# One load instead of two at the end of a streamed mixture of softmaxes, and a store and a wait moved by one step

## The chip, the core and the metric

The kernel runs on one core of one Trainium2 chip. The metric is the device time of one execution in microseconds (us); less is better. Engines are named as in the profile: ACT (ScalarE) computes the exponentials, DVE (VectorE) the weighted sums, POOL (GpSimd) one small product for each group of heads, and SP (SyncE) issues most of the transfers. The transfers themselves run on 16 DMA engines that all queues share.

## The reference

The input `logits` has 32 x 128 rows of 4 heads by 4096 values in float32 (268.4 MB); `prior` has 4 values for each row. Each row's four softmaxes are mixed with weights that are themselves a softmax:

```python
prior_probs = np.exp(prior - prior.max(axis=-1, keepdims=True))
prior_probs = prior_probs / prior_probs.sum(axis=-1, keepdims=True)
softmax = np.exp(logits - logits.max(axis=-1, keepdims=True))
softmax = softmax / softmax.sum(axis=-1, keepdims=True)
mixture = np.sum(prior_probs[..., None] * softmax, axis=2)
```

The output has 4096 rows of 4096 float32 values (67.1 MB). The kernel takes the exponentials without the subtraction of the maximum.

## The kernel before

The 4096 rows are cut into U = 32 units of 128 rows, one row in each partition. A unit's logits are 64 KB in each partition, 16 KB for each of the H = 4 heads. All of the order is written by hand: in the function `only`, an instruction keeps just the waits that are handed to it, so each engine executes its list in the order of the program, and what it waits for can be read from the calls.

**Loads.** `load(u)` (L94 to L109) is issued from SP into `ltile[:, u % 2]`, one of two buffers. Most units come as one transfer of 64 KB per partition. Unit 0 and the last three come in parts, set by `cuts`: two parts of 32 KB (two heads each), and for the last unit one part of 32 KB and two of 16 KB. The first part of unit u's load waits for the first weighted sum of unit u-2 (`adds[u - 2, 0]`), any further part for an exponential of unit u-2. It is issued at the end of the loop's turn for unit u-2.

**Exponentials.** `exp(h)` (L158) is one ACT instruction for each head, with the sum over the row as a second output. Head 0 is written in place, heads 1 to 3 into `ebuf1`, `ebuf2` and `ebuf3`, of which there is one each; so exponential h of unit u waits for the sum of head h of unit u-1. In the last two units all four are written in place.

**Weights.** `weigh(h, n)` (L167 to L173) takes the reciprocal of n sums on DVE and multiplies it on POOL by the prior's weight. In units 0 to 27 it is called once, for all four heads, behind the fourth exponential; in units 28 to 31 twice, for two heads each.

**Sums.** `add(h)` (L175 to L187) is one DVE instruction for each head: head 0 writes `obuf[:, u % 2]`, the others add to it. In the last two units the result stays in `ltile`. The last sum of unit 31 is cut into two halves, each followed by a store of its half.

**Stores.** `store(u - 1)` (L112 to L114) writes 2 MB. For u - 1 up to 27 it stands in ACT's list, in the loop's turn for unit u, ahead of the third exponential (h = 2), and waits for the last sum of unit u-1. The stores of units 28 to 31 are issued from SP, behind all loads.

**The wait for a free output buffer.** `obuf` has two halves, so unit u's sums may start only when the store of unit u-2 has landed. `free` holds that store. In units 2 to 27 it is handed to the fourth exponential (L197), in units 28 and 29 to the first `weigh`, that is to POOL's product.

Of the kernel before, what the change touches and what calls it, by code (L numbers as in the profile page):

```python
# [37 lines left out]
@with_exitstack  # L38
def kernel(
    ctx: ExitStack,  # L40
    tc: tile.TileContext,
    logits: bass.AP,
    prior: bass.AP,
    out: bass.AP,
):
    nc = tc.nc
    nc.at_finalize(early_first_load)
    B, S, H, V = logits.shape
    assert prior.shape == (B, S, H)
    assert out.shape == (B, S, V)  # L50
    P = 128
    J = 2
    R = P * J
    G = B * S // R
    U = G * J
    assert G * R == B * S and G <= 32 and H == 4

    lg = logits.rearrange("b s h v -> (b s) h v").rearrange("(g p j) h v -> g j p h v", p=P, j=J)
    ov = out.rearrange("b s v -> (b s) v").rearrange("(g p j) v -> g j p v", p=P, j=J)
    pv = prior.rearrange("b s h -> (b s) h").rearrange("(g r) h -> g r h", r=R)  # L60

    cpool = ctx.enter_context(tc.tile_pool(name="cpool", bufs=1))
    psum = ctx.enter_context(tc.tile_pool(name="psum", bufs=1, space=bass.MemoryType.PSUM))

    before = {}

    def only(ins, *keep):
        for k in keep:  # L70
            tc.add_manual_dep(
                ins.ins,
                k.ins.name,
                mybir.DependencyInfo(mybir.DependencyClass.Sync, mybir.DependencyReason.DATA),
                reason="all that this instruction waits for",
            )
        tc.declare_no_dep(
            ins.ins,
            group="loop",
            keep=[k.ins for k in keep] + before.get(ins.ins.engine, []),  # L80
            reason="covered by the waits that are kept",
        )
        tc.add_to_no_dep_group("loop", ins.ins)
        before[ins.ins.engine] = [ins.ins]
        return ins


    ltile = cpool.tile([P, 2, H, V], FP32, name="ltile")
    loads = {}
    exps = {}  # L90
    adds = {}
    stores = {}

    def load(u):  # L94
        if u == 0 or u >= U - 3:
            cuts = (0, 2, 3, 4) if u == U - 1 else (0, 2, 4)
        else:
            cuts = (0, H)
        for h, to in zip(cuts, cuts[1:]):
            ld = nc.sync.dma_start(  # L100
                out=ltile[:, u % 2, h:to], in_=lg[u // J, u % J, :, h:to, :]
            )


            if u >= 2:
                only(ld, adds[u - 2, 0] if h == 0 else exps[u - 2, to - 1])
            else:
                only(ld)
            for k in range(h, to):  # L109
                loads[u, k] = ld  # L110

    def store(u, acc, eng, lo=0, hi=V):  # L112
        st = eng.dma_start(out=ov[u // J, u % J, :, lo:hi], in_=acc[:, lo:hi])  # L113
        stores[u] = only(st, adds[u, H - 1])  # L114


    pr = cpool.tile([G, R, H], FP32, name="pr")
    pn = cpool.tile([32, H, R], FP32, name="pn")
    pmax = cpool.tile([G, R], FP32, name="pmax")
    pp = cpool.tile([P, J, H, 32], FP32, name="pp")  # L120


    dsum = cpool.tile([P, U, H], FP32, name="dsum")
    rden = cpool.tile([P, U, H], FP32, name="rden")
    coeff = cpool.tile([P, U, H], FP32, name="coeff")

    ebuf1 = cpool.tile([P, V], FP32, name="ebuf1")
    ebuf2 = psum.tile([P, V], FP32, name="ebuf2")  # L130
    ebuf3 = cpool.tile([P, V], FP32, name="ebuf3")
    obuf = cpool.tile([P, 2, V], FP32, name="obuf")

    with tc.manual_schedule():
        load(0)
        nc.scalar.dma_start(out=pr, in_=pv)
        load(1)
        nc.gpsimd.memset(pn, 0.0)  # L138
        nc.vector.reduce_max(pmax, pr, axis=AX.X)  # L139
        nc.vector.tensor_sub(pr, pr, pmax.unsqueeze(2).to_broadcast([G, R, H]))  # L140
        nc.scalar.activation(pr, pr, AF.Exp)  # L141
        nc.vector.reduce_sum(pmax, pr, axis=AX.X)  # L142
        nc.vector.reciprocal(pmax, pmax)  # L143
        nc.vector.tensor_mul(  # L144
            pn[0:G].rearrange("g h r -> g r h"), pr, pmax.unsqueeze(2).to_broadcast([G, R, H])
        )
        pq = pn.rearrange("g h (p j) -> g j h p", j=J)
        for t in range(P // 32):
            nc.vector.transpose(pp[32 * t : 32 * (t + 1)], pq[:, :, :, 32 * t : 32 * (t + 1)])  # L149

        for u in range(U):
            bufd = u < U - 2
            lt = ltile[:, u % 2]
            acc = obuf[:, u % 2] if bufd else lt[:, 0]
            es = (lt[:, 0], ebuf1, ebuf2, ebuf3) if bufd else [lt[:, h] for h in range(H)]
            ppu = pp[:, u % J, :, u // J]

            def exp(h, *keep):  # L158
                ex = nc.scalar.activation(  # L159
                    es[h], lt[:, h], AF.Exp, accum_out=dsum[:, u, h : h + 1]  # L160
                )
                keep = (loads[u, h],) + keep
                if bufd and h and u:
                    keep += (adds[u - 1, h],)
                exps[u, h] = only(ex, *keep)

            def weigh(h, n, *keep):  # L167
                rc = nc.vector.reciprocal(rden[:, u, h : h + n], dsum[:, u, h : h + n])  # L168
                only(rc, exps[u, h + n - 1])
                mul = nc.gpsimd.tensor_mul(  # L170
                    coeff[:, u, h : h + n], rden[:, u, h : h + n], ppu[:, h : h + n]
                )
                return only(mul, rc, *keep)  # L173

            def add(h, mul, lo=0, hi=V):  # L175
                if h == 0:
                    st = nc.vector.tensor_scalar(  # L177
                        out=acc[:, lo:hi], in0=es[h][:, lo:hi], scalar1=coeff[:, u, h : h + 1],
                        scalar2=None, op0=ALU.mult,
                    )  # L180
                    adds[u, h] = only(st, mul)
                else:
                    st = nc.vector.scalar_tensor_tensor(  # L183
                        out=acc[:, lo:hi], in0=es[h][:, lo:hi], scalar=coeff[:, u, h : h + 1],
                        in1=acc[:, lo:hi], op0=ALU.mult, op1=ALU.add,
                    )
                    adds[u, h] = only(st, mul, adds[u, h - 1])  # L187

            free = (stores[u - 2],) if bufd and u >= 2 else ()

            m = H if u < U - 4 else 2
            for h in range(H):
                if h == 2 and 0 < u < U - 3:
                    store(u - 1, obuf[:, (u - 1) % 2], nc.scalar)
                exp(h, *(free if m == H and h == H - 1 else ()))  # L197
                if (h + 1) % m:
                    continue
                g = h + 1 - m  # L200
                mul = weigh(g, m, *(free if m < H and g == 0 else ()))
                for k in range(g, h + 1):
                    n = 2 if u == U - 1 and k == H - 1 else 1
                    w = V // n
                    for c in range(n):
                        add(k, mul, c * w, (c + 1) * w)
                        if n > 1:
                            store(u, acc, nc.sync, c * w, (c + 1) * w)
            if u + 2 < U:
                load(u + 2)  # L210
            if u == U - 3:
                store(u - 1, obuf[:, (u - 1) % 2], nc.sync)
                store(u, acc, nc.sync)
            elif u == U - 2:
                store(u, acc, nc.sync)
# [30 lines left out]
```

## Time and profile before

| | before |
|---|---|
| median of 3 runs (lowest to highest) | 780.94 us (780.91 to 780.97) |
| profiled execution's own time | 780.97 us |
| its span, first to last instruction | 779.2 us |
| DVE busy | 521.0 us (67%) |
| ACT busy | 469.8 us (60%) |
| POOL busy | 8.4 us (1%) |
| bytes read and written | 268.50 MB and 67.11 MB, 431 GB/s over the span |
| DMA queue q1 (SP's) | 82.3% of the 16 engines' span |
| DMA queue q10 (ACT's) | 17.6% of the 16 engines' span |

The span is taken from the first instruction to the last; the profiled execution's own time is 1.8 us longer. Busy time counts what an engine computes, not what its sequencer issues or waits for. The share of a DMA queue is the time that its packets took, over the span and 16 engines; both queues run on the same engines, so their shares add.

### The profile page before, as it was taken

To read this page: it belongs to the slowest core of one execution; us is meant where nothing else is said; L and a number is where in the kernel's file an instruction comes from. 1 tells how busy PE (TensorE), PEld (TensorE's weight loads), DVE (VectorE), ACT (ScalarE), POOL (GpSimd) and SP (SyncE) were. 2 spreads that over 40 slices of the span, in tenths; PEclk is the share of its full clock that TensorE was granted. 3 is DMA by queue.
4 is the path that set the end of the run, shared out by engine and by line. 5 is a ranking of instruction groups with operands and counts; after the bars stand their busy time and mean duration, and the time that the engine had idled before them with its cause. 6 is when DMAs were issued, how large, how long until landed. Compare 5 with 4: busy or idle time off the path is not lost.

```text
span 779.2 us, 628 instructions
## 1 busy us (share of the span) xinstructions
DVE 521.0 (67%) x174; ACT 469.8 (60%) x258; POOL 8.4 (1%) x41
## 2 busy tenths in 40 slices
DVE  4447865568655686556875558755577555788986
ACT  4376565765557655577555675546755567557782
POOL 0000000000000000000000000000000000000000
DMA  9999999999999999999999999999999999999998
GB/s 407 458 417 402 473 404 447 414 471 418 408 463 404 461 417 440 435 451 410 434 451 407 458 405 467 421 416 446 429 446 417 463 399 463 410 429 431 432 432 376
DMA packets 10116, 335.65 MB, mean 431 GB/s; under 512 B 1136, under 2 KB 1136, under 8 KB 1152
## 3 DMA queue, kind: packets, MB, share of 16 engines
q1 hardware_dynamic: 6048, 276.83, 82.3%
q10 hardware_dynamic: 4064, 58.79, 17.6%
q14 instruction: 4, 0.03, 0.0%
HBM read 268.50 MB, written 67.11 MB: 431 GB/s over the span
## 4 chain that ended last, share of the span: by engine, by line
DVE 55%; ACT 26%; DMA 15%; issue 2%; ACTq 1%; POOL 1%; DVEq 0%; SPq 0%; POOLq 0%
DVE obuf L183 45%; ACT ebuf L159 24%; DMA ltile<-in_logits_dram 9%; DVE obuf L177 8%; DMA out_dram<-obuf 6%; ACT ltile L159 1%; ACTq L113 1%; DVE ltile L183 1%; POOL coeff L170 1%; DVE rden L168 1%; DVEq L241 0%; SPq L100 0%; POOLq L241 0%; POOLq L170 0%
## 5 line engine op out<-in xcount | busy, mean ns | idle before, releaser
L183 DVE SCALAR_TENSOR_TENSOR obuf<-ebuf,coeff,obuf 128x4096 f32<-128x4096 f32 x90 | 403.6, 4484 | 3.8 <-POOL coeff L170 0.6
L159 ACT ACTIVATE ebuf<-ltile 128x4096 f32<-128x4096 f32 x90 | 323.6, 3595 | 43.4 <-DVE obuf L183 36.0
L159 ACT ACTIVATE ltile<-ltile 128x4096 f32<-128x4096 f32 x38 | 137.3, 3614 | 241.5 <-DMA ltile<-in_logits_dram 241.5
L168 DVE RECIPROCAL rden<-dsum 128x4 f32<-128x4 f32 (+1 forms) x36 | 6.3, 174 | 227.1 <-ACT ebuf L159 224.4
L177 DVE TENSOR_SCALAR obuf<-ltile,coeff 128x4096 f32<-128x4096 f32 x30 | 70.6, 2354 | 11.0 <-POOL coeff L170 11.0
L183 DVE SCALAR_TENSOR_TENSOR ltile<-ltile,coeff 128x4096 f32<-128x4096 f32 (+1 forms) x7 | 27.0, 3874 | 0.8 <-POOL coeff L170 0.6
L159 ACT ACTIVATION_READ_ACCUMULATOR ebuf<-ltile 128x1 f32 x90 | 16.8, 186 | 0.0
L170 POOL TENSOR_TENSOR coeff<-rden,pp 128x4 f32<-128x4 f32 (+1 forms) x36 | 7.2, 201 | 755.2 <-DVE rden L168 744.5
L159 ACT ACTIVATION_READ_ACCUMULATOR ltile<-ltile 128x1 f32 x38 | 7.1, 186 | 0.0
L139 DVE TENSOR_REDUCE pmax<-pr 16x256 f32<-16x1024 f32 x1 | 1.2, 1207 | 7.7 <-DMA pr<-in_prior_dram 7.7
L141 ACT ACTIVATE pr<-pr 16x1024 f32<-16x1024 f32 x1 | 1.1, 1055 | 7.7 <-DVE pr L140 7.7
L177 DVE TENSOR_SCALAR ltile<-ltile,coeff 128x4096 f32<-128x4096 f32 x2 | 4.7, 2354 | 0.6 <-POOL coeff L170 0.6
L144 DVE TENSOR_TENSOR pn<-pr,pmax 16x1024 f32<-16x1024 f32 x1 | 1.9, 1941 | 0.1
L141 ACT ACT_TABLE_LOAD x1 | 1.3, 1283 | 1.2 <-PEq L230 1.2
L142 DVE TENSOR_REDUCE pmax<-pr 16x256 f32<-16x1024 f32 x1 | 1.2, 1207 | 1.1 <-ACT pr L141 1.1
L149 DVE STREAM_TRANSPOSE pp<-pn 32x256 f32<-32x256 f32 x4 | 1.7, 435 | 0.1
L143 DVE RECIPROCAL pmax<-pmax 16x256 f32<-16x256 f32 x1 | 1.7, 1741 | 0.0
L140 DVE TENSOR_TENSOR pr<-pr,pmax 16x1024 f32<-16x1024 f32 x1 | 1.2, 1211 | 0.0
L138 POOL MEMSET pn<- 32x1024 f32 x1 | 0.9, 942 | 0.3 <-POOLq L230 0.3
L230 POOL MEMSET const-bfloat16-1.0<- 128x1 bf16 x1 | 0.1, 107 | 0.0
L230 POOL MEMSET const-uint8-127<- 128x1 uint8 x1 | 0.1, 107 | 0.0
L230 POOL MEMSET const-float32-0.0<- 128x1 f32 x1 | 0.1, 104 | 0.2 <-issue 0.2
(1 smaller groups left out, 0.1 us busy)
## 6 DMA issues: line engine op xcount, KB each, us to landing
out_dram<-obuf ACTq DMA_DIRECT2D x28, 2048.0 KB, 27.9
ltile<-in_logits_dram SPq DMA_DIRECT2D x7, 4096.0 KB, 25.5
ltile<-in_logits_dram SPq DMA_DIRECT2D x2, 2048.0 KB, 30.9
out_dram<-obuf SPq DMA_DIRECT2D x2, 2048.0 KB, 33.9
out_dram<-ltile SPq DMA_DIRECT2D x1, 2048.0 KB, 17.2
out_dram<-ltile SPq DMA_DIRECT2D x2, 1024.0 KB, 4.8
ltile<-in_logits_dram SPq DMA_DIRECT2D x28, 29.5
pr<-in_prior_dram ACTq DMA_DIRECT2D x1, 64.0 KB, 6.9
```

What stands on the lines that cost most here:

```text
L113: st = eng.dma_start(out=ov[u // J, u % J, :, lo:hi], in_=acc[:, lo:hi])
L139: nc.vector.reduce_max(pmax, pr, axis=AX.X)
L140: nc.vector.tensor_sub(pr, pr, pmax.unsqueeze(2).to_broadcast([G, R, H]))
L141: nc.scalar.activation(pr, pr, AF.Exp)
L143: nc.vector.reciprocal(pmax, pmax)
L144: nc.vector.tensor_mul(pn[0:G].rearrange("g h r -> g r h"), pr, pmax.unsqueeze(2).to_broadcast([G, R, H]))
L149: nc.vector.transpose(pp[32 * t : 32 * (t + 1)], pq[:, :, :, 32 * t : 32 * (t + 1)])
L159: ex = nc.scalar.activation(es[h], lt[:, h], AF.Exp, accum_out=dsum[:, u, h : h + 1])
L168: rc = nc.vector.reciprocal(rden[:, u, h : h + n], dsum[:, u, h : h + n])
L170: mul = nc.gpsimd.tensor_mul(coeff[:, u, h : h + n], rden[:, u, h : h + n], ppu[:, h : h + n])
L177: st = nc.vector.tensor_scalar(out=acc[:, lo:hi], in0=es[h][:, lo:hi], scalar1=coeff[:, u, h : h + 1], scalar2=None, op0=ALU.mult,)
L183: st = nc.vector.scalar_tensor_tensor(out=acc[:, lo:hi], in0=es[h][:, lo:hi], scalar=coeff[:, u, h : h + 1], in1=acc[:, lo:hi], op0=ALU.mu ...
```

## The change

Three edits. The last unit's second half (heads 2 and 3) is loaded as one part of 32 KB per partition instead of two of 16 KB. In units 1 to 28 the store of the unit before stands in ACT's list ahead of the fourth exponential instead of the third. And in units 2 to 27 the wait for the store of unit u-2 goes from the fourth exponential to POOL's product in `weigh`; the fourth exponential waits instead for the store of unit u-4, from unit 4 on. In units 28 and 29 that wait was at `weigh` already.

```diff
     def load(u):
         if u == 0 or u >= U - 3:
-            cuts = (0, 2, 3, 4) if u == U - 1 else (0, 2, 4)
+            cuts = (0, 2, 4)
         else:
             cuts = (0, H)
...
             free = (stores[u - 2],) if bufd and u >= 2 else ()
 
             m = H if u < U - 4 else 2
             for h in range(H):
-                if h == 2 and 0 < u < U - 3:
+                late = h == H - 1 and 4 <= u < U - 3
+                if h == H - 1 and 0 < u < U - 3:
                     store(u - 1, obuf[:, (u - 1) % 2], nc.scalar)
-                exp(h, *(free if m == H and h == H - 1 else ()))
+                exp(h, *((stores[u - 4],) if late else ()))
                 if (h + 1) % m:
                     continue
                 g = h + 1 - m
-                mul = weigh(g, m, *(free if m < H and g == 0 else ()))
+                mul = weigh(g, m, *(free if g == 0 else ()))
```

## The prediction

> **What bounds the kernel now.** I read the page's list of DMA queues first, then the chain of waits, then stretches of the middle and of the end, and last the order of instructions in one unit and in the last unit.
>
> The page: queues (packets, MB, share of 16 engines), then the chain that ended last.
>
> ```profile
> q1 hardware_dynamic: 6048, 276.83, 82.3%
> q10 hardware_dynamic: 4064, 58.79, 17.6%
> ...
> DVE 55%; ACT 26%; DMA 15%; issue 2%; ACTq 1%; POOL 1%; DVEq 0%; SPq 0%; POOLq 0%
> ```
>
> The two readings disagree. The chain puts 81% on DVE and ACT; the queues add to 99.9% of the span. A chain follows whatever released an instruction last, and in a loop where every transfer is issued early that is an engine even if the data set the pace. The stretches decide (after the interval: its length, busy DVE, ACT, POOL, clock, DMA share, GB/s):
>
> ```profile
> 306.30:330.46 24.16, 15.98 (x6) 14.61 (x8) 0.20 (x1) 1.00 1.00 434
> 330.46:354.63 24.17, 15.99 (x6) 14.61 (x8) 0.20 (x1) 1.00 1.00 434
> ...
> 676.00:756.00 80.00, 65.22 (x24) 58.41 (x33) 1.39 (x7) 1.00 1.00 429
> ...
> 777.00:778.00 1.00, 0.00 (x0) 0.00 (x0) 0.00 (x0) 1.00 0.14 57
> ```
>
> Each unit takes 24.16 us, which is its 8.39 MB of load and 2.10 MB of store at 434 GB/s with a DMA share of 1.00; DVE and ACT each rest for over 8 us of it. The share falls only in the last 2 us. So the time is the data's time, and an edit counts only where it lets the DMA engines run dry. One unit of the middle (start, duration, engine, line; idle before and its releaser in brackets):
>
> ```profile
> 306.30 3.62 ACT L159 ACTIVATE ltile<-ltile 128x4096 f32<-128x4096 f32 x1 [8.17 <-DMA ltile<-in_logits_dram]
> ...
> 314.60 0.34 ACTq L113 DMA_DIRECT2D out_dram<-obuf  x1
> 314.99 3.59 ACT L159 ACTIVATE ebuf<-ltile 128x4096 f32<-128x4096 f32 x1 [1.38 <-DVE obuf L183]
> ...
> 322.82 2.35 DVE L177 TENSOR_SCALAR obuf<-ltile,coeff 128x4096 f32<-128x4096 f32 x1 [0.32 <-POOL coeff L170]
> ```
>
> The unit's load lands at 306.28, ACT stops 1.38 us at the store, the first sum ends at 325.2. That sum releases the load after next, 18.9 us into the unit, while the next load still has 5.2 us of data to come: SP's queue never empties. And the last unit:
>
> ```profile
> 749.12 3.62 ACT L159 ACTIVATE ltile<-ltile 128x4096 f32<-128x4096 f32 x1 [2.41 <-DMA ltile<-in_logits_dram]
> 752.74 3.60 ACT L159 ACTIVATE ltile<-ltile 128x4096 f32<-128x4096 f32 x1
> 756.34 3.60 ACT L159 ACTIVATE ltile<-ltile 128x4096 f32<-128x4096 f32 x1
> 759.94 3.60 ACT L159 ACTIVATE ltile<-ltile 128x4096 f32<-128x4096 f32 x1
> ...
> 764.20 9.14 DVE L183 SCALAR_TENSOR_TENSOR ltile<-ltile,coeff 128x4096 f32<-128x4096 f32 x3 [0.31 <-POOL coeff L170]
> ```
>
> Four exponentials run without a gap from the landing of the first half, then the sums of heads 2 and 3 and the two stored halves.
>
> **Part 1, the store behind the third exponential.** The store needs the last sum of the unit before (done at 314.57, 8.3 us into the unit). Today it blocks ACT's list until then, 1.38 us in each of 26 units (36.0 us in the waits). Behind the change the third exponential needs only that unit's third sum, done 4.5 us earlier, so ACT's four exponentials run on end, the reciprocal comes 1.4 us earlier, and with it all sums and the load's issue (lead 6.6 us instead of 5.2). The store is not later for that: its sum is 1.4 us earlier, at 6.9 us into the unit, and the third exponential starts at 7.2. ACT's sequencer issues a store while an exponential ahead of it runs (the first store, 46.07, lies inside the one from 45.25 to 48.76), so I expect it between 6.9 and 7.3; if it waits for the third exponential's end, 10.9. Either way the DMA engines have the next load queued, so the price is 0; the cover is the 5.2 us of lead.
>
> **Part 2, the wait for the store of unit u-2, from ACT to POOL.** That store lands at 318.35, 12.1 us into the unit: it is queued behind the one before, and the landings are 24.17 us apart whenever it is issued. POOL's product will be ready at 16.3 - 1.4 = 14.9. So the wait has 2.8 us to spare. Behind it on POOL is nothing but the next product; DVE's four sums wait for it, behind them SP's load and ACT's store. If the store were held to 10.9, the first one at 52.4 instead of 46.1, its landings would come at about 16.4, the product would wait 1.5 us and stand where it is today (16.3): still 0. The wait for the store of unit u-4 is met two units earlier: 0.
>
> **Part 3, the last load.** The two 2 MB parts are issued at 723.77 and 727.37 and land 30.2 and 31.5 us later, at 753.99 and 758.88, 4.89 us apart: back to back, at 429 GB/s. One 4 MB part lands at 758.9, since it is the same data in the same queue behind the same transfers, and no edit changes the bytes ahead of it. What is lost is the early landing of head 2. Its exponential starts at 756.34 today and would start at 758.90. In the unit before, the same two exponentials after a stall (739.40) are followed by the sum 7.82 us after their start (747.22). So the sum of head 2 starts at 758.90 + 7.82 = 766.72 instead of 764.20: 2.52 us later. DVE's sums of heads 0 and 1 end at 763.82 and so hide nothing. The last two stores are issued at 773.62 and 775.89 instead of 771.10 and 773.37.
>
> What of the 2.52 us reaches the end? The store of unit 30 lands at 773.46, so before the change the queue is just full: the first half's packets start 0.83 us after its issue, as the engines come free. Now the engines stand empty for a while. The last halves took 4.76 and 4.92 us from issue to landing, 2.41 us apart, with some DMA engines up to 1 us behind the others (landings from 774.81 to 775.87). Bounds:
> - Lowest: the lag of those engines vanishes in the empty stretch. 773.62 + 0.83 to the first packets + 4.84 of data (2.10 MB at 433 GB/s) + 0.35 from an engine's last data to its landing = 779.64, against 778.28 today: +1.36.
> - The issue shifts and the 4.92 us stays: 775.89 + 4.92 = 780.81, +2.53.
> - Highest, by the trace's only large transfer into an empty queue, the very first load: 12.52 us for data that take 9.72 elsewhere, 2.80 over. 773.62 + 2.80 + 4.84 = 781.26, +2.98.
>
> I take +2.0, between the first two, nearest to the halves' own rows: an empty queue removes the lag but costs a slower first packet (the first load's first packets took 1.2 to 2.1 us, later ones 1.21). The packets' own saving is nothing: 128 of 32 KB at 1213 ns instead of 256 of 16 KB at 611 ns is 9 ns for each, 0.07 us on an engine.
>
> The Trainium skill, "DMA: Bandwidth & Descriptors", section "Rules for kernel authors", asks for fewer and larger transfers, and its section "Anatomy of one DMA — SWDGE (gpsimd) path" puts a fixed cost of about 2.0 us on each. By that rule the merged load alone would give 2.0 us back, and the time would be no worse than today's. The 4.89 us between the two landings show no such cost, so I let the row decide.
>
> **Sum.** 0 + 0 + 2.0 on a span of 779.2 gives 781.2; the profiled execution's own time of 780.97, which is 0.03 over the median of the runs, becomes 783.0.
>
> **The rivals.**
> - *The engines set the pace (faster).* If the chain's 81% were the truth, ACT's 1.38 us would come off 26 units: 36 us, some 747. It decides as soon as the DMA share in the middle lies under 1.00; a share of 0.99 would give 0.01 x 24.16 x 26 = 6 us, 777. The chain speaks for it, the share and 24.16 = 10.49 MB / 434 GB/s against. 0.04.
> - *The end is shorter than I think (no change).* The delay is 2.52 at the issue, but the sum at the lower bound is +1.36, under the 0.2% (1.56 us) that a measurement of this kernel can tell from no change. It decides where the final halves need less than 3.95 us after the issue of the last one. For it: the lagging engines. Against: the first packet's start. 0.16, 782.3.
> - *The wait on POOL runs the load queue dry (much slower).* It decides when a store lands over 21.5 us into its unit (14.9 plus the lead of 6.6); each us beyond costs 26 us, so 809 for the first. The landings lie at 12.1 and at worst at 16.4. 0.03.
> - *The change doesn't do what it says:* in ACT's list the store is later, in time hardly. That is in part 1 and costs nothing.
>
> **How the numbers follow.** My forecast has 0.77, at 783.0 within 782.5 to 784.0 (+1.56 to +2.98). The no-change case adds 782.3 below it (+1.36, and 0.1 for the runs). The range is 782.2 to 784.0; the two extreme rivals, 0.07, are left out with some of the edges. Slower: 0.77 + 0.03 = 0.80; same 0.16; faster 0.04.
>
> **What would show it.** Right: ACT's 36.0 us behind DVE's sums fall to a few; the reciprocal lies 14.6 us behind the unit's first exponential, not 16.0; units stay at 24.16 us with a share of 1.00; POOL waits for a store only in units 28 and 29; the third exponential of the last unit starts at 758.9 with 2.5 us of idle time behind a load; the DMA share dips between 772 and 775; the last sums start near 766.7. Wrong: a unit shorter than 24.1 us (engines bound), a DMA share under 0.99 in the middle (the new wait), a landing of the last load before 757, or a span under 780.6.

## The result and the profile after

| | before | after |
|---|---|---|
| median | 780.98 us (780.91 to 781.09, 6 runs) | 783.06 us (782.94 to 783.17, 6 runs) |
| ratio, with 95% interval | | 1.0026 (1.0014 to 1.0039) |
| span of the profiled execution | 779.2 us | 781.3 us |
| DVE / ACT busy | 521.0 / 469.8 us | 521.1 / 466.8 us |

The changed kernel is 2.1 us slower. The page of after, DMA queues (packets, MB, share) and the chain that ended last:

```profile
q1 hardware_dynamic: 5904, 276.83, 82.0%
q10 hardware_dynamic: 4064, 58.79, 17.6%
...
DMA 64%; ACT 27%; DVE 6%; issue 2%; POOL 0%; DVEq 0%; POOLq 0%
```

The bytes are the same; the 144 packets fewer of q1 are the joined rows and one DMA's semaphore writes. The chain has changed its nature: DVE fell from 55% to 6%, and DMA rose from 15% to 64%. Stretches of after (length, DVE, ACT, POOL, clock, DMA share, GB/s):

```profile
306.30:330.46 24.16, 15.98 (x6) 14.51 (x8) 0.20 (x1) 1.00 1.00 434
...
676.00:756.00 80.00, 64.00 (x23) 58.20 (x33) 1.39 (x7) 1.00 1.00 429
...
772.50:773.00 0.50, 0.50 (x1) 0.00 (x0) 0.00 (x0) 1.00 0.00 0
773.00:773.50 0.50, 0.50 (x2) 0.00 (x0) 0.00 (x0) 1.00 0.00 0
773.50:774.00 0.50, 0.50 (x2) 0.00 (x0) 0.00 (x0) 1.00 0.00 0
774.00:774.50 0.50, 0.50 (x1) 0.00 (x0) 0.00 (x0) 1.00 0.59 246
```

Until 756 the data move at the same rate as before. Then comes a hole that was not there: from 772.5 to 774 no DMA packet starts while DVE is still summing. The kernel before had packets there:

```profile
772.00:774.00 2.00, 1.34 (x1) 0.00 (x0) 0.00 (x0) 1.00 0.99 410
```

One unit of the middle, timeline of after:

```profile
306.37 3.62 ACT L159 ACTIVATE ltile<-ltile 128x4096 f32<-128x4096 f32 x1 [9.66 <-DMA ltile<-in_logits_dram]
...
313.18 0.34 ACTq L113 DMA_DIRECT2D out_dram<-obuf  x1
...
313.58 3.56 ACT L159 ACTIVATE ebuf<-ltile 128x4096 f32<-128x4096 f32 x1
...
321.40 2.35 DVE L177 TENSOR_SCALAR obuf<-ltile,coeff 128x4096 f32<-128x4096 f32 x1 [0.32 <-POOL coeff L170]
```

The store is issued 6.83 us behind the landing of the unit's load (306.35), earlier than before (8.3), though it stands later in ACT's list; the third exponential follows without a stop, and the first sum starts 1.4 us earlier. The last unit, timeline of after:

```profile
752.73 3.60 ACT L159 ACTIVATE ltile<-ltile 128x4096 f32<-128x4096 f32 x1
...
758.82 3.62 ACT L159 ACTIVATE ltile<-ltile 128x4096 f32<-128x4096 f32 x1 [2.40 <-DMA ltile<-in_logits_dram]
...
762.44 3.60 ACT L159 ACTIVATE ltile<-ltile 128x4096 f32<-128x4096 f32 x1
...
766.64 9.14 DVE L183 SCALAR_TENSOR_TENSOR ltile<-ltile,coeff 128x4096 f32<-128x4096 f32 x3 [0.31 <-POOL coeff L170]
```

The last load lands at 758.80 (758.88 before), the third exponential waits 2.40 us for it, the sums of heads 2 and 3 start 2.44 us later (766.64 for 764.20). The two last stores are issued at 773.54 and 775.80 and land at 777.42 and 780.29; before they landed at 775.87 and 778.28. So 2.44 us at the issue became 2.01 us at the landing.

### The profile page after: what moved, and what is told of

It is laid out like the page before. It is cut to its first block, busy times and chain, and to the rows that moved or that the text cites. A ratio compares the mean times of both kernels' runs of the same rounds, so it can differ in the third digit from the quotient of the medians.

```text
span 781.3 us, 652 instructions
## 1 busy us (share of the span) xinstructions
DVE 521.1 (67%) x174; ACT 466.8 (60%) x258; POOL 8.4 (1%) x41
## 4 chain that ended last, share of the span: by engine, by line
DMA 64%; ACT 27%; DVE 6%; issue 2%; POOL 0%; DVEq 0%; POOLq 0%
DMA ltile<-in_logits_dram 62%; ACT ebuf L159 19%; ACT ltile L159 8%; DVE obuf L177 5%; DMA out_dram<-obuf 2%; DVE ltile L183 1%; POOL coeff L170 0%; DVE rden L168 0%; DVEq L240 0%; POOLq L240 0%; POOLq L170 0%
```

## The experiments

The theory behind the prediction, called A below: all of the loss is at the end, because the last stores find an empty queue; the two edits of the middle cost nothing, because the loads are issued early.

**1 and 2: each half of the change alone.**

```diff
 e1_merged_load_only, against the kernel before
-            cuts = (0, 2, 3, 4) if u == U - 1 else (0, 2, 4)
+            cuts = (0, 2, 4)
```

> The kernel before with the first edit alone: the last unit's second half as one 32 KB part; store and wait stay where they were. Theory A (the whole loss comes from the end, because the last stores find an empty queue): 783.1, +2.1 us, with the third exponential of the last unit at 758.8 and the DMA share falling to 0 between 772 and 774. Rival B (the moved store and wait cost part of it): less than +1.5 us, 782.4 or below. Rival C (the moved store and wait give time in the middle that hides a larger loss at the end): more than +2.5 us, 783.5 or above.

```diff
 e2_moved_waits_only, against the changed kernel
-            cuts = (0, 2, 4)
+            cuts = (0, 2, 3, 4) if u == U - 1 else (0, 2, 4)
```

> The changed kernel with the last unit's second half in two 16 KB parts again; the moved store and the moved wait alone. Theory A: the time before, 781.0 within 0.2 us, though ACT's wait for DVE (36.0 us in the kernel before) is gone and the loads are issued 1.4 us earlier in each unit. Rival B: 781.5 to 782.5. Rival C: below 780.5.

Measured: 783.17 us for the load alone, ratio 1.0027 (1.0016 to 1.0038), and 781.03 us for the moved store and wait, ratio 1.0000 (0.9991 to 1.0009). The same stretch of each, first of the merged load alone, then of the moved store and wait alone:

```profile
772.00:774.00 2.00, 2.00 (x2) 0.00 (x0) 0.00 (x0) 1.00 0.04 16
```

```profile
772.00:774.00 2.00, 1.33 (x1) 0.00 (x0) 0.00 (x0) 1.00 1.01 418
```

The hole comes with the merged load alone, and the time with it. Rivals B and C fall. In the second run ACT no longer waits for DVE at all, 36.0 us of waiting gone, and the time is what it was: its wait for loads ahead of the first exponentials rose instead, from 241.5 to 280.3 us.

**3 and 4: a cover for the end.** The changed kernel (run 3), and the changed kernel with the last load split as in run 2 (run 4), get 2 MB more to load behind the store of unit 30, into a buffer that is no longer read.

```diff
             elif u == U - 2:
                 store(u, acc, nc.sync)
+                fill = nc.sync.dma_start(out=ebuf1, in_=lg[0, 0, :, 0, :])
+                only(fill, adds[U - 3, 1])
```

> The changed kernel with one more 2 MB load behind the store of unit 30, into a buffer that nobody reads any more, so that the DMA engines have 4.84 us more of data when the last stores are issued. Theory A (the loss is the time in which the queue is empty): the late third exponential is covered, so the time is that of the kernel before plus the data, 781.0 + 4.8 = 785.8, and equal to the next run within 0.2 us. Rival D (the larger part costs time by itself, in landing or in the sums behind it): 2 us above the next run, 787.9.

> The same extra 2 MB load, with the last unit's second half in two 16 KB parts. Theory A and rival D: 781.0 + 4.8 = 785.8; theory A puts the run before at the same time, rival D 2 us above. Anything under 785 would say that the end was not bound by the data in the kernel before.

Measured: 786.25 us, ratio 1.0067 (1.0054 to 1.0079), with the merged load; 786.44 us, ratio 1.0069 (1.0056 to 1.0082), with the two parts. The extra load cost 5.3 to 5.5 us over the kernel before, a little more than its 4.84 us of data, in both; what the rest is was not tried. The 2.1 us between the two cuts are gone: with data in the queue, last stores that are issued 2.4 us later (773.44 for 771.04) cost nothing, so rival D falls. The stretch that was empty, merged load with the cover:

```profile
772.00:774.00 2.00, 2.00 (x2) 0.00 (x0) 0.00 (x0) 1.00 0.92 393
```

**5 and 6: more parts, and one.**

```diff
 e5_four_parts
-            cuts = (0, 2, 4)
+            cuts = (0, 1, 2, 3, 4) if u == U - 1 else (0, 2, 4)
 e6_one_part: the load waits for the last exponential of unit 29 too
-            cuts = (0, 2, 4)
+            cuts = (0, H) if u == U - 1 else (0, 2, 4)
```

> The changed kernel with the last unit loaded in four parts of 16 KB. Its exponentials can start 4.8 us earlier and follow the parts, the last one at 758.9 instead of 762.4; DVE's sums of heads 0 and 1 start about 0.6 us earlier and the last stores are issued about 3.5 us earlier than in the changed kernel. Theory A (the end is the data's end once the queue stays full): 780.8 to 781.0, no more than 0.2 us under the kernel before, since the DMA engines were empty there for only some 0.2 us. Rival E (the end follows the compute chain, whatever the queue holds): 1 us under the kernel before, 780.0.

> The changed kernel with the last unit's 64 KB as one part, so all four exponentials wait for the landing at 758.8. The chain of the last unit is then 4 exponentials (14.4 us), a weight (0.5 us) and the sums of heads 2 and 3 and stores. Theory A: with the queue empty every us of delay counts in full; the fourth exponential ends at 773.3, and DVE, which starts the sum of head 0 at 766.6 and ends head 1 at 773.5, starts head 2 at 773.9, so 7.3 us behind the changed kernel: 790.3. A theory in which the DMA engines still hide a part of it as in the change (2.0 of 2.5): under 789.

Measured: 780.89 us for four parts, ratio 0.9999 (0.9990 to 1.0008), no gain over the kernel before; the last stores were issued 2.76 us earlier than in the changed kernel, not 3.5, since DVE was still at the sums of heads 0 and 1. That is only 0.32 us earlier than in the kernel before (770.78 for 771.10), a step that the run times cannot tell from nothing. The profiles can: the last landing comes 4.83 us behind that of unit 30's store in both runs, the time that 2.10 MB need at 434 GB/s. One part took 790.31 us: 7.25 us over the changed kernel, for last stores that are issued 7.31 us later (780.85 for 773.54). With runs 3 and 4 these show a knee. In front of it, where the queue is full, an earlier issue is worth nothing; rival E falls mainly by runs 3 and 4, where 2.4 us at the issue changed nothing. Behind it each us counts in full. Only in the change itself, which crosses the knee, did part of the delay vanish.

**7 and 8: how much delay the middle hides.** The first sum of units 2 to 27 is computed more than once, with the same result. EXTRA stands for 1 in run 7 and for 3 in run 8.

```diff
                     for c in range(n):
+                        for _ in range(EXTRA if k == 0 and 2 <= u < U - 4 else 0):
+                            add(0, mul)
                         add(k, mul, c * w, (c + 1) * w)
```

> The changed kernel with the first sum of units 2 to 27 computed twice, which adds 2.4 us on DVE between the weight and the issue of the load after next. Theory A (a lead of 6.6 us covers delays in the middle): lead 4.2 us, time unchanged at 783.1 within 0.3 us. Theory F (the engines' chain sets the pace): 26 x 2.4 = 62 us more, 845.

> The changed kernel with the first sum of units 2 to 27 computed four times, 7.1 us more on DVE in each (23.1 of 24.2 us busy). Theory A: the load is issued 24.8 us after the landing of the unit, 0.6 us behind the landing of the next one, and needs 1 to 2 us to start, so the engines stand empty of loads for 1.6 to 2.6 us in each unit, partly filled by the store in flight: 20 to 65 us more, 805 to 850. Theory F: 26 x 7.1 = 185 us more. If the time stays at 783, the lead is not what covers the middle.

Measured: 783.69 us with one extra sum and 873.64 us with three. The first is 0.63 us over the changed kernel, twice what was allowed. It does not lie in the middle, where units still take 24.16 us at 434 GB/s. The last load landed at 759.46 instead of 758.80: its first DMA engine was no later than in the changed kernel (757.68), its last one lagged more. That lag, the spread over a load's 16 landings, stepped from 1.21 us to 1.98 at the load that landed at 694.19, and was 1.78 at the last load (1.04 in the changed kernel). An 8 KB packet of the instruction queue (q14) had started at 692.8; whether it is the cause was not tried, so the cause of the 0.63 us stays open. The second is 90 us more, above the upper bound of 65, so theory A gave the wrong price. Timeline of the run with three extra sums:

```profile
458.62 3.59 ACT L159 ACTIVATE ebuf<-ltile 128x4096 f32<-128x4096 f32 x1 [0.81 <-DVE obuf L183]
...
463.14 0.34 ACTq L113 DMA_DIRECT2D out_dram<-obuf  x1
463.52 3.62 ACT L159 ACTIVATE ebuf<-ltile 128x4096 f32<-128x4096 f32 x1 [1.19 <-DVE obuf L183]
...
467.76 9.52 DVE L177 TENSOR_SCALAR obuf<-ltile,coeff 128x4096 f32<-128x4096 f32 x4 [0.32 <-POOL coeff L170]
```

None of these lines waits for a load. The unit's first exponential does (446.13, not shown), but when it has ended, at 449.75, the second still waits for DVE until 454.10. The fourth exponential waits for the last sum of the unit before (its buffer, and the store ahead of it), the weight for that exponential, the next sums for the weight: a closed loop of 27.74 us (440.02 to 467.76). Take off the three extra sums (9.52 - 2.37 = 7.15) and the loop of the changed kernel has 20.6 us. Its slack against the data's 24.17 is 3.6 us, and not the 6.6 us by which the loads are early. Theory G says so; in the kernel before, the same loop took in the third exponential as well, and should have had no slack at all.

**9 and 10: lead or loop.** EXTRA is 2 in the changed kernel (run 9) and 1 in the kernel before (run 10), with the edit shown above.

> The changed kernel with the first sum of units 2 to 27 computed three times, 4.7 us more on DVE in each. Theory G (from the run with three extra sums: the middle has a closed loop, DVE's four sums, then the fourth exponential that needs the last of them, then weight and first sum; 27.7 us there, so 20.5 us in the changed kernel, and the slack of the middle is 24.2 - 20.5 = 3.6 us): 20.5 + 4.7 = 25.3 us for each unit, 1.1 above the data's 24.2, times 26: 28 us more, 811. Theory A as predicted (the slack is the 6.6 us by which the loads are issued early): 1.9 us left, the time stays at 783 to 784.

> The kernel before, with the first sum of units 2 to 27 computed twice, 2.4 us more on DVE in each; the changed kernel took 783.7 with the same addition. Theory G: in the kernel before the loop runs over the third exponential too, since the store stood ahead of it and waits for the last sum: sums 15.9, store 0.4, two exponentials 7.3, weight 0.5, in all 24.17 us, which has no slack against the data's 24.17. So 26 x 2.4 = 62 us more, 842 to 843. Theory A as predicted (a lead of 5.2 us covers it): 781 to 782.

Measured: 812.57 us, ratio 1.0404 (1.0387 to 1.0421), and 840.86 us, ratio 1.0765 (1.0749 to 1.0781). Loads are issued 25.34 us apart in the first (390.70, 416.04) and 26.55 us apart in the second (378.02, 404.57); theory G had 25.3 and 24.17 + 2.37 = 26.54. The first sums of two units in a row, timeline of run 9 and then of run 10:

```profile
408.88 7.13 DVE L177 TENSOR_SCALAR obuf<-ltile,coeff 128x4096 f32<-128x4096 f32 x3 [0.32 <-POOL coeff L170]
...
434.22 7.13 DVE L177 TENSOR_SCALAR obuf<-ltile,coeff 128x4096 f32<-128x4096 f32 x3 [0.32 <-POOL coeff L170]
```

```profile
399.80 4.74 DVE L177 TENSOR_SCALAR obuf<-ltile,coeff 128x4096 f32<-128x4096 f32 x2 [0.32 <-POOL coeff L170]
...
426.36 4.74 DVE L177 TENSOR_SCALAR obuf<-ltile,coeff 128x4096 f32<-128x4096 f32 x2 [0.32 <-POOL coeff L170]
```

What runs out first in the middle is the loop's slack, and not the lead: in run 9 a load is still issued 1.3 us before the one ahead of it lands (390.70 and 392.03), and yet the unit is 1.17 us longer. The same extra sum that costs the kernel before 60 us costs the changed kernel 0.6.

## Why the prediction was right, and where its reasons were not

**Part 3 was right in each step up to the issue of the last stores.** 783.0 was predicted and 783.06 measured. The third exponential started at 758.82 (758.90 predicted), the sums at 766.64 (766.72), the last stores were issued at 773.54 and 775.80 (773.62 and 775.89). For the end the prediction had three prices, +1.36, +2.53 and +2.98, and took +2.0 between the first two. That was a choice and no sum; that the landing moved by 2.01 is luck to that precision, while the two bounds held.

Where the 2.01 us come from can be read from the landings on the 16 DMA engines. The first half needed 3.88 us from its issue into an empty queue, and its landings were 0.16 us apart (777.26 to 777.42) where they had been 1.05 us apart: the lag went, as the lower bound had it. The last half then took 4.49 us, with 15 of its landings from 779.73 to 779.97 and one at 780.29. Its first landing moved by 2.43 us, as much as its issue; its spread fell from 0.98 to 0.56 us. So 0.43 us of the issue's 2.44 vanished with the lag.

Two reasons given for the end did not hold. A slower first packet in an empty queue does not show in these stores: their first packets took 0.31 to 0.32 us in both kernels. And the 0.83 us from the issue to the first packet were put down to the engines coming free, with the queue "just full"; they are 0.83 us in the empty queue too (773.54 to 774.37), and 1.11 us with four parts, where the queue was full. So in the kernel before the first engines already stood idle for a moment: it lies at the knee, not in front of it.

**The rule that stood against it.** The Trainium skill, "DMA: Bandwidth & Descriptors", says less than the prediction took from it. Its section "Rules for kernel authors" asks to coalesce many small transfers and calls those under 64 KB mostly overhead; the parts here have 2 MB. The fixed cost of about 2.0 us in its section "Anatomy of one DMA — SWDGE (gpsimd) path" is fitted to transfers issued from GpSimd; these are issued from SP. The saving of 2.0 us that the prediction estimated from them does not show: merging cost 2.2 us by itself (783.17 for 780.97), and four parts (780.89) were no slower than the kernel before with three (780.98). In the backed-up queue here the next part's data followed at once (landings 4.89 us apart, 429 GB/s), and what a cut buys is an earlier landing.

**Parts 1 and 2 were right in the sum, wrong in the cover.** The stall of 36.0 us went, the store was issued at 6.83 us (6.9 to 7.3 predicted), the price was 0. The 16.4 us for the landing of a later store follow from no row; the store was not late, so nothing rested on them. The cover was named wrongly: a delay in the middle meets the loop's slack of 3.6 us before it meets the lead of 6.6 us. And the step "a chain follows whatever released an instruction last, and in a loop where every transfer is issued early that is an engine even if the data set the pace" dismissed a true reading. Chain of waits of before, one unit (start, us, what):

```profile
298.65 2.37 DVE obuf L177
...
310.08 4.50 DVE obuf L183
...
314.60 0.34 ACTq L113
...
314.99 7.32 ACT ebuf L159 x4
...
322.82 2.37 DVE obuf L177
```

From first sum to first sum, 24.17 us, no piece of it is a transfer: a loop that closes on itself. That it has no slack is shown by run 10, where 2.37 us more on DVE made the unit 2.38 us longer. The data need 24.17 us as well: with the loop shortened, loads still land 24.17 us apart (330.52, 354.70, 378.87). The kernel before was bound by both at once. The same part of the chain of after:

```profile
275.43 30.91 DMA ltile<-in_logits_dram
...
306.37 3.71 ACT ltile L159 x2
310.08 10.80 ACT ebuf L159 x6
...
321.40 2.37 DVE obuf L177
...
323.78 30.91 DMA ltile<-in_logits_dram
```

Now each unit's chain ends in a load, and the engines follow the data. So the change did free the engines, by 24.17 - 20.6 = 3.6 us in each unit, and gained nothing since the data were exactly as long. The rival that the engines set the pace was half true: its mechanism was there, its gain of 36 us was not, because a second bound stood at the same place.

**Its test was wrong too.** "It decides as soon as the DMA share in the middle lies under 1.00". The changed kernel with two extra sums, bound by its engines:

```profile
300.00:500.00 200.00, 162.82 (x56) 115.97 (x63) 1.62 (x8) 1.00 1.00 413
```

The share is 1.00 and the rate 413 GB/s instead of 434. What tells is the rate.

**A small miss.** POOL was to wait for a store in units 28 and 29; it did so once, for 10.0 us (10.7 before).

## What to carry to other kernels

At the end of a stream of data, ask when the queue runs empty against when the last stores are issued: in front of that point an earlier issue was worth nothing here, behind it each us counted, so the last load should be in parts just small enough that the engines' chain ends inside the queued data. Where a chain of waits goes round a whole period without a transfer, its length is a bound of its own; compare it with the data's time, since shortening it below that buys slack and no time. Slack is measured by adding delay: one doubled instruction for each unit told two kernels whose times are 2.1 us apart from each other by 57 us.

## What the runs showed of the hardware

A DMA share of 1.00 does not prove that the queue is full. In the run with two extra sums a quarter of the 64 KB packets took over 2.64 us, where in the kernels before and after nearly all took 2.418 us; a packet counts as busy however slowly it moves, so the share hides what the rate shows. All three runs whose loop is longer than the data's 24.17 us show such packets, 27 to 28% of them in the kernel before with one extra sum and in the changed kernel with three (shares 0.97 and 0.93); in the changed kernel with one extra sum they are 0.1%. Why they are slower was not tried.

A stored 1 MB issued into an empty queue landed 3.88 us after its issue in the changed kernel, and 3.88 to 3.90 us in five other runs (4.24 us in a sixth): 2.42 us of data and some 1.5 us around them, 0.83 us of it ahead of the first packet.

The 16 DMA engines do not stay in step. In the kernel before, the spread over a load's 16 landings is 0.37 us at 160.5, 0.72 at 185.1, 1.06 at 209.6, and it steps again from 0.98 to 1.30 at 524.2. Ahead of each step stands an 8 KB packet of the instruction queue, at 175.0, 193.8 and 514.1. This goes together in time; no run tries it as a cause.
